# Stick-breaking heads of a hybrid block: turned weights in other PSUM banks and first in each step, two gates behind the last head, one causal select for both parts

## The chip, the cores and the metric

The kernel runs on one core of one Trainium2 chip. The metric is the device time of one execution in microseconds. Names of engines: PE multiplies matrices (PEld is its queue of weight loads, which overlaps it), DVE is the vector engine, ACT the scalar engine, POOL is GpSimd, and SP issues most DMAs. PSUM has eight banks of 128 x 512 fp32 values; matmuls write there, and ACT and DVE read it.

## What is computed

One transformer block over 512 tokens with a model width of 1024: a modulated RMS norm, then two mixers side by side (retention with 4 heads, stick-breaking attention with 16 heads of width 64), their gated sum, an output projection, a modulated feed-forward part, and a final norm. The stick-breaking mixer, retention's scores and the merge are what matters here:

```python
def stick_breaking_attention(q, k, v):
    scale = SB_HEAD_DIM ** -0.5
    for i in range(s_len // BLOCK):                  # 4 blocks of 128 queries
        end = (i + 1) * BLOCK
        z = jnp.einsum('bhtd,bhsd->bhts', qb, kb).astype(jnp.float32) * scale
        mask = s_pos[None, :] < t_pos[:, None]
        log_1m_beta = jnp.where(mask, jax.nn.log_sigmoid(-z), 0.0)
        after = lax.cumsum(log_1m_beta, axis=3, reverse=True) - log_1m_beta
        log_a = jax.nn.log_sigmoid(z) + after
        a = jnp.where(mask, jnp.exp(log_a), 0.0)
        outs.append(jnp.einsum('bhts,bhsd->bhtd', a.astype(v.dtype), vb))
...
    decay_mask = jnp.where(diff >= 0, jnp.exp(jnp.maximum(diff, 0.0) * log_gamma[:, None, None]), 0.0)
    scores = jnp.einsum('bhncd,bhnmd->bhncm', qc, kc) * decay_mask[None, :, None]
...
    g_sb, g_ret = jnp.split(jax.nn.sigmoid(br + b_branch[l]), N_BRANCH, axis=-1)
    merged = (g_sb * jnp.einsum('bse,ed->bsd', o_sb, w_proj_sb[l])
              + g_ret * jnp.einsum('bse,ed->bsd', o_ret, w_proj_ret[l]))
```

## The kernel before

Every fp32 matrix is held as two parts of a rounded type, `hi` and `lo`, and a product is three matmuls (hi hi, hi lo, lo hi). `split` (L204) makes the parts: ACT writes `hi` (L206), DVE the difference `lo` (L208, or L209 with a scale). Activations are kept with the features in the 128 partitions and the 512 tokens in the free dimension. Weights come by DMA as `raw` tiles of 128 x 1024 and are split into `whi` and `wlo`. A product of 512 x 1024 activations with 128 columns of weights (`gemm`) is 24 matmuls of 512 columns into one bank.

PSUM has three pools: `ps` with four banks, `z` with three, `av` with one. A tile of a pool can be written again once the readers of the tile that had the bank before it are done.

**Order.** The program issues instructions through a framework that orders each engine's queue by a model of when operands are there; so neighbouring pieces of code interleave in a queue. `issue_after` holds back what is in its block until the named instruction has been placed.

**Retention.** A head's scores are made by `ret_scores` (L708) into the three `z` banks, in four blocks of columns from the table `GEO`: key block j against the queries from j onward. Entry j = 3 had a block of 256 columns, of which the first 128 lie above the diagonal; both parts of every block are made by `split` (ACT, then DVE), and then `causal` (L587) sets what lies above the diagonal to zero on POOL by `affine_select` (L592): for each of three banks, hi and lo apart, 128 columns at the bank's start, and for bank 2 also 256 columns that hold j = 3's zeroed half and its diagonal block. That is eight selects a head, thirty-two in all. `ret_out` (L739) then multiplies the blocks with the values, bank by bank of the output (`z`, `z`, `z`, `av`), in matmuls that read the selected tiles. For head 0 this stands right behind the making of the sums for the later split products by `sv_acts`, a long row of DVE additions over SBUF tiles (L878, L889).

**Stick-breaking.** Sixteen heads run one behind the other in the loop over `heads(h)` (L1087); step h holds these pieces:

- `sb_front(h)`: eight matmuls of q and k into three `z` banks (two each of 512, 384, 256 and 128 columns), then eight sigmoids on ACT (L627) from these banks into SBUF: 1 - beta into `n4`, `n1`, beta into `b4`, `b1` (the tiles s and t of one of two `stick_sets`)
- `sb_turn(h - 1)`: ten PE transposes (L643) of the weights of the head before, 128 x 128 each, into three further `z` tiles, and three splits of them (ACT L206, DVE L208) into `s` tiles
- `sb_scan(h)`: DVE's products along the row, a scan of 1024 and one of 256 columns (L633) and the multiplications by beta (L634); issued behind the last split of `sb_turn`
- `sb_out(h - 1)`: eight matmuls of values and turned weights into the `av` bank, a copy out by ACT (L663), a DMA that moves 64 partitions to the other half (`t<-t`, L665), and an addition (L666) into the tile `o_sb`

Beside these, each step has work for PE that depends on no head: an odd h up to 11 has `mix(1)`, one gate of 24 matmuls (`gate`, its sigmoid `g<-ps` at L808); an even h up to 10 has `sb_qk(p)`, 48 matmuls that make q and k of two later heads; h = 12 to 15 have `mix(2)`, and h = 16, which has only the turn and the output of head 15, has none left. I call these gate steps, qk steps and two-gate steps. Behind the loop, `acts` splits the eight `o_sb` tiles, and the projection of the stick-breaking mixer multiplies all of them (`gemm(o, weight(("ps", d)), acts)`).

The order of the three pieces that use `z` banks is front, turn, next front; so three banks carry six tiles a step.

Of the kernel before, what the change touches and what calls it, by code (L numbers as in the profile page):

```python
# [15 lines left out]
ALU = mybir.AluOpType  # L16
# [3 lines left out]
P = 128  # L20
# [83 lines left out]
SM_BADA, SM_G1, SM_G2, SM_GF, SM_BB, SM_C, SM_N = 0, 48, 56, 64, 72, 88, 96  # L104


GEO = ((0, 0, 0, 512), (1, 0, 128, 384), (2, 0, 256, 256), (2, 256, 256, 256))


SEG = ((0, 1, 384, 896), (1, 2, 0, 0), (2, 1, 0, 512), (3, 0, 0, 0))  # L110
# [5 lines left out]
def kernel(  # L116
# [9 lines left out]
    nc = tc.nc  # L126
# [9 lines left out]
    def nm(s):  # L136
        uid[0] += 1
        return f"{s}_{uid[0]}"

    def ps():  # L140
        return pspool.tile([P, S], F32, tag="ps", bufs=BUFS["ps"], name=nm("ps"))

    def psa():
        return pspool.tile([P, S], F32, tag="av", bufs=BUFS["av"], name=nm("av"))

    def psz():
        return pspool.tile([P, S], F32, tag="z", bufs=BUFS["z"], name=nm("z"))

    def pair(tag):
        return apool.tile([P, 2, S], F32R, tag=tag, bufs=BUFS[tag], name=nm(tag))  # L150

    def tmp():
        return apool.tile([P, S], F32, tag="t", bufs=BUFS["t"], name=nm("t"))

    def otile():
        return apool.tile([P, S], F32, tag="o", bufs=BUFS["o"], name=nm("o"))
# [21 lines left out]
    for j in range(KT):  # L178
# [13 lines left out]
                            channel_multiplier=-1)  # L192
# [11 lines left out]
    def split(dst_hi, dst_lo, src, scale=1.0, eng=None):  # L204

        nc.scalar.activation(dst_hi, src, AF.Copy, scale=scale)  # L206
        if isinstance(scale, float) and scale == 1.0:
            return (eng or nc.vector).tensor_sub(dst_lo, src, f(dst_hi))  # L208
        return nc.vector.scalar_tensor_tensor(  # L209
            dst_lo, src, scale, f(dst_hi), op0=ALU.mult, op1=ALU.subtract  # L210
        )
# [15 lines left out]
    def mm(o, lhs, rhs, start, stop):  # L227
        return nc.tensor.matmul(o, lhs, rhs, start=start, stop=stop, skip_group_check=True).ins  # L228

    def mm3(o, lh, ll, rh, rl, start, stop):  # L230
        mm(o, lh, rh, start, False)
        mm(o, lh, rl, False, False)
        mm(o, ll, rh, False, stop)
# [206 lines left out]
    with tc.manual_schedule(engines={nc.vector.engine, nc.scalar.engine, nc.tensor.engine}):  # L440

        nc.scalar.preload_act_table_set("natural_log_exp_and_others")
        c = sm[:, SM_C : SM_C + KT]
# [137 lines left out]
    def sb_qk(p):  # L581
        qp, kp = ps(), ps()
        gemm(qp, weight(("sq", p)), hs)
        gemm(kp, weight(("sk", p)), hs)
        sb_qk_store(p, qp, kp)

    def causal(t, bank):  # L587

        op = ALU.is_ge

        def sel(ap, n, base):
            nc.gpsimd.affine_select(  # L592
                ap, ap, pattern=[[1, n]], compare_op=op, fill=0.0, base=base,
                channel_multiplier=-1,
            )

        sel(t[:, 0:P], P, 0)
        if bank == 2:
            sel(t[:, 256:512], 256, -P)

    def sticks():

# [10 lines left out]
    def sb_front(h):  # L613
        q, k = sbq[h], sbk[h]
        z = [psz(), psz(), psz()]
        for i, bank, c, _ in reversed(SEG):
            w = (i + 1) * P
            for n in range(2):
                head_pe[h] = mm(z[bank][:, c : c + w], q[:, n, i * P : (i + 1) * P], k[:, 0:w],
                                n == 0 and c == 0, n == 1)  # L620
        n4, n1, b4, b1 = stick_sets[h % 2]
        for segs in ((3,), (2, 0), (1,)):
            for (t4, t1), scale in (((n4, n1), -1.0), ((b4, b1), 1.0)):
                for i, bank, c, at in (SEG[i] for i in segs):
                    w = (i + 1) * P - 1
                    t = t1 if i == 1 else t4
                    nc.scalar.activation(t[:, at : at + w], z[bank][:, c : c + w], AF.Sigmoid, scale=scale)  # L627
        return n4, n1, b4, b1

    def sb_scan(n4, n1, b4, b1):  # L630
        for n, b, d in ((n4, b4, diag), (n1, b1, diag[:, 640:896])):
            w = n.shape[-1]
            nc.vector.tensor_tensor_scan(n[:, ::-1], n[:, ::-1], d[:, ::-1], 0.0, op0=ALU.mult, op1=ALU.max)  # L633
            nc.vector.tensor_mul(b[:, 0 : w - 1], b[:, 0 : w - 1], n[:, 1:w])  # L634

    def sb_turn(n4, n1, b4, b1):
        at = [psz(), psz(), psz()]
        for i, _, _, a in reversed(SEG):
            t = b1 if i == 1 else b4
            for j in range(i + 1):  # L640
                bank, c = TGEO[j]
                c += (i - j) * P
                nc.tensor.transpose(at[bank][:, c : c + P], t[:, a + j * P : a + (j + 1) * P], ident)  # L643
        avs = []
        for bank in range(3):
            w = TBANKW[bank]
            hl = pair("s")
            ins = split(hl[:, 0, :w], hl[:, 1, :w], at[bank][:, :w])
            avs.append(hl)
        return avs, ins  # L650

    def sb_out(h, avs):
        vt = sbv[h // 4]
        o = psa()
        r, hf = (h % 4) // 2, h % 2
        for j in (3, 2, 1, 0):
            bank, c = TGEO[j]
            w = S - j * P
            v = vt[j // 2][:, j % 2, r * 256 + hf * P : r * 256 + hf * P + P]
            for i in range(2):  # L660
                mm(o[:, j * P : S], v, avs[bank][:, i, c : c + w], j == 3 and i == 0, j == 0 and i == 1)
        u, u2 = tmp(), tmp()
        nc.scalar.activation(u, o, AF.Copy)  # L663
        own, oth = (slice(0, HD), slice(HD, P)) if hf == 0 else (slice(HD, P), slice(0, HD))
        nc.sync.dma_start(u2[own], u[oth])  # L665
        nc.vector.tensor_add(o_sb[h // 2][own], u[own], u2[own])  # L666
# [41 lines left out]
    def ret_scores(h, qk):  # L708
        q1, q2, k1, k2 = qk
        z = [psz(), psz(), psz()]  # L710
        st = {}
        for j in (3, 2, 1, 0):
            bank, c, t0, w = GEO[j]
            js = slice(j * P, (j + 1) * P)
            for n, (q, k) in enumerate(((q1, k1), (q2, k2))):
                mm3(z[bank][:, c : c + w], k[:, 0, js], k[:, 1, js], q[:, 0, t0:S], q[:, 1, t0:S],
                    n == 0 and j != 2, n == 1)
        for j in (3, 2, 1, 0):
            bank, c, t0, w = GEO[j]
            if bank not in st:  # L720
                st[bank] = pair("s")
            hl = st[bank]
            split(hl[:, 0, c : c + w], hl[:, 1, c : c + w], z[bank][:, c : c + w],
                  gk[:, h * 4 + j : h * 4 + j + 1])
        for bank in (2, 1, 0):
            for i in range(2):
                causal(st[bank][:, i, :], bank)
        return st

    def ret_scale(h, ssq):  # L730
# [8 lines left out]
    def ret_out(h, st, vt):  # L739
# [3 lines left out]
        for b, o in enumerate(banks):  # L743
            for j in range(b + 1):
                bank, c, t0, _ = GEO[j]
                at = c + b * P - t0
# [297 lines left out]
    qk = ret_qk(0, qk_ps)  # L1044
    vt = ret_v(v_ps)
    st = ret_scores(0, qk)
    sgs = ret_silu(0)
    steps = sv_acts()
# [4 lines left out]
    for h in range(3):  # L1053
        ys = ret_gate(h, *outs, sgs)
        qk = ret_qk(h + 1)
        st, outs = {}, []
        vt = lambda: [rvts[b] for b in range(4)]
        seven(("vg", h + 1), h, lambda: ys, rv_store, lambda: st.update(ret_scores(h + 1, qk)),
              lambda: outs.extend(ret_out(h + 1, st, vt())))
        sgs = [rsgs[b] for b in range(4)]  # L1060
# [6 lines left out]
    def sb_v(g):  # L1067

        sbv[g] = [pair("v") for _ in PI]
        for n, vt in enumerate(sbv[g]):  # L1070
            nc.sync.dma_start(f(vt), vspill[2 * (g - 2) + n])

    sbv.update({g: [vts[g, n] for n in PI] for g in PI})
    mixes = [(ret_mix, d) for d in range(8)] + [(sb_mix, d) for d in range(8)]

    def mix(n):
        for _ in range(n):
            fn, d = mixes.pop(0)
            fn(d)
# [5 lines left out]
    fronts = {}  # L1085

    def heads(h):  # L1087
        with tc.issue_after(act_table.ins):
            ins = act_table
            if h < 16:  # L1090
                fronts[h] = sb_front(h)
            if h:
                if h % 8 == 1 and h > 8:
                    sb_v(2)
                    sb_v(3)
                avs, ins = sb_turn(*fronts.pop(h - 1))
            if h < 16:
                with tc.issue_after(ins.ins):
                    sb_scan(*fronts[h])
            if h:  # L1100
                if h % 2:
                    o_sb[h // 2] = otile()
                sb_out(h - 1, avs)

    for h in range(17):
        heads(h)
        p = h // 2 + 2
        if p > 7:
            mix(min(2, len(mixes)))
        elif h % 2:  # L1110
            mix(1)
        else:
            sb_qk(p)
# [7 lines left out]
    for d in range(8):  # L1121
        o = ps()
        gemm(o, weight(("ps", d)), acts)
        r, t = tmp(), tmp()
# [5 lines left out]
        ins = split(hl[:, 0, :], hl[:, 1, :], t)  # L1130
# [596 lines left out]
```

## Time and profile before

| | us |
|---|---|
| median of 3 runs | 1130.73 (1130.22 to 1131.09) |
| the profiled execution's own time | 1131.71 |
| its span, first to last instruction | 1129.8 |
| heads, first front to the last output | about 474 to 687 in the span |

The profile's mean granted PE clock is 0.997 of full speed. One row of the instruction timeline is: start in us, duration in us, engine, line, operation, output and inputs by the program's names, partitions x elements, count; in brackets the engine's idle time before it and what ended it. A row that stands for several instructions of one kind has their common duration. PE's durations overlap (a matmul's end is modelled and includes its way through the array), so what a matmul costs is read from start to start.

### The profile page before, as it was taken

To read this page: it belongs to the slowest core of one execution; us is meant where nothing else is said; L and a number is where in the kernel's file an instruction comes from. 1 tells how busy PE (TensorE), PEld (TensorE's weight loads), DVE (VectorE), ACT (ScalarE), POOL (GpSimd) and SP (SyncE) were. 2 spreads that over 40 slices of the span, in tenths; PEclk is the share of its full clock that TensorE was granted. 3 is DMA by queue.
4 is the path that set the end of the run, shared out by engine and by line. 5 is a ranking of instruction groups with operands and counts; after the bars stand their busy time and mean duration, and the time that the engine had idled before them with its cause. 6 is when DMAs were issued, how large, how long until landed. Compare 5 with 4: busy or idle time off the path is not lost.

```text
span 1129.8 us, 15925 instructions
## 1 busy us (share of the span) xinstructions
PE 1112.0 (98%) x6096; PEld 958.7 (85%) x6096; DVE 837.8 (74%) x1174; ACT 554.1 (49%) x863; POOL 65.9 (6%) x94
## 2 busy tenths in 40 slices
PE   8999999999999999999999999999999999999996
PEld 6887888888888888877777777889999999999986
DVE  7898856959968958476777765767996777667656
ACT  5445445435434644355555553357655444444333
POOL 0031000011021010000000000000000000000000
PEclk9999999999999999999999999999999999999998
DMA  9714432766776476867675448762556564564322
GB/s 357 297 56 150 146 115 87 224 133 209 233 159 224 141 162 237 219 172 203 163 203 164 124 129 297 249 185 57 151 186 165 171 169 112 149 186 132 92 77 75
DMA packets 63147, 190.90 MB, mean 169 GB/s; under 512 B 7776, under 2 KB 9824, under 8 KB 63072
## 3 DMA queue, kind: packets, MB, share of 16 engines
q1 hardware_dynamic: 55760, 171.02, 47.1%
q0 software_dynamic: 6768, 18.35, 9.5%
q8 instruction: 48, 0.79, 0.3%
q10 hardware_dynamic: 544, 0.52, 0.1%
q14 instruction: 27, 0.22, 0.1%
HBM read 146.35 MB, written 16.78 MB: 144 GB/s over the span
## 4 chain that ended last, share of the span: by engine, by line
PE 86%; DVE 5%; ACT 3%; DMA 3%; issue 2%; POOL 1%; SPq 0%; DVEq 0%; ACTq 0%
PE ps L228 65%; PE z L228 15%; PE av L228 3%; PE z L643 2%; ACT s L627 1%; POOL s L592 1%; DMA araw<-wada 1%; DVE araw L256 1%; DMA sraw<-wada 1%; ACT g L808 1%; DVE wlo L859 1%; DVE wlo L208 0%; DMA q<-qp 0%; DVE t L766 0%; DMA t<-t 0%
## 5 line engine op out<-in xcount | busy, mean ns | idle before, releaser
L228 PE MATMUL ps<-h,whi 128*128 128x512 f32 (+1 forms) x1154 | 339.9, 376 | 0.0
L228 PEld LDWEIGHTS ps<-h,whi 128*128 128x128 f32 x1154 | 209.1, 189 | 34.7 <-issue 0.5
L228 PE MATMUL ps<-h,wlo 128*128 128x512 f32 (+1 forms) x577 | 215.3, 377 | 0.0
L206 ACT ACTIVATE whi<-raw 128x1024 fp32r<-128x1024 f32 (+1 forms) x104 | 108.5, 1044 | 183.2 <-PE ps L228 137.4
L208 DVE TENSOR_TENSOR wlo<-raw,whi 128x1024 fp32r<-128x1024 f32 (+1 forms) x104 | 125.0, 1203 | 72.8 <-ACT whi L206 72.0
L228 PE MATMUL ps<-s,whi 128*128 128x512 f32 x480 | 148.8, 391 | 1.4 <-ACT s L206 1.0
L228 PEld LDWEIGHTS ps<-h,wlo 128*128 128x128 f32 x577 | 108.9, 189 | 17.1
L228 PE MATMUL z<-q,whi 128*128 128x256 f32 x504 | 106.8, 283 | 0.0
L228 PEld LDWEIGHTS ps<-s,whi 128*128 128x128 f32 x480 | 89.3, 188 | 20.1 <-ACT s L206 1.5
L859 DVE TENSOR_TENSOR wlo<-s,whi 128x1024 fp32r<-128x1024 f32 x46 | 56.1, 1223 | 53.2 <-ACT whi L855 53.1
L228 PE MATMUL ps<-s,wlo 128*128 128x512 f32 x240 | 93.5, 389 | 0.0
L228 PEld LDWEIGHTS z<-q,whi 128*128 128x128 f32 x504 | 84.9, 192 | 1.5
L855 ACT ACTIVATE whi<-s 128x1024 fp32r<-128x1024 f32 x47 | 49.7, 1057 | 59.0 <-PE ps L228 48.5
L228 PE MATMUL ps<-whi,h 128*128 128x512 f32 x222 | 71.4, 391 | 0.0
L1168 DVE SCALAR_TENSOR_TENSOR o<-ps,mod,o 128x512 f32<-128x512 f32 (+1 forms) x63 | 42.5, 681 | 33.7 <-PE ps L228 33.6
L208 DVE TENSOR_TENSOR s<-z,s 128x512 fp32r<-128x512 f32 (+1 forms) x60 | 33.6, 614 | 27.6 <-ACT s L206 27.6
L228 PEld LDWEIGHTS ps<-s,wlo 128*128 128x128 f32 x240 | 45.1, 188 | 9.4
L855 ACT ACTIVATE whi<-raw 128x1024 fp32r<-128x1024 f32 x28 | 29.6, 1058 | 47.0 <-PE ps L228 45.2
L228 PEld LDWEIGHTS ps<-whi,h 128*128 128x128 f32 x222 | 41.6, 188 | 9.5 <-ACT t L999 0.6
L228 PE MATMUL ps<-q,whi 128*128 128x256 f32 (+1 forms) x224 | 49.3, 314 | 0.0
L228 PE MATMUL z<-qp,whi 128*128 128x256 f32 x168 | 47.3, 283 | 0.0
L228 PE MATMUL z<-q,wlo 128*128 128x256 f32 x168 | 46.4, 283 | 0.0
(320 smaller groups left out, 2127.2 us busy)
## 6 DMA issues: line engine op xcount, KB each, us to landing
raw<-wp SPq DMA_DIRECT2D x145, 512.0 KB, 4.0
araw<-wada SPq DMA_DIRECT2D x32, 512.0 KB, 4.0
araw<-wp SPq DMA_DIRECT2D x30, 512.0 KB, 4.3
s<-wp SPq DMA_DIRECT2D x24, 512.0 KB, 6.1
sraw<-wada SPq DMA_DIRECT2D x16, 512.0 KB, 8.6
q<-qp SPq DMA_DIRECT2D x32, 256.0 KB, 3.7
spill<-o POOLq DMA_DIRECT2D x24, 256.0 KB, 5.0
o<-xT SPq DMA_DIRECT2D x16, 256.0 KB, 4.1
```

The lines of the kernel that those rows point to most:

```text
L206: nc.scalar.activation(dst_hi, src, AF.Copy, scale=scale)
L208: return (eng or nc.vector).tensor_sub(dst_lo, src, f(dst_hi))
L228: return nc.tensor.matmul(o, lhs, rhs, start=start, stop=stop, skip_group_check=True).ins
L256: nc.vector.scalar_tensor_tensor(raw, raw, 1.0, cact, op0=ALU.mult, op1=ALU.mult, accum_out=col)
L592: nc.gpsimd.affine_select(ap, ap, pattern=[[1, n]], compare_op=op, fill=0.0, base=base, channel_multiplier=-1,)
L627: nc.scalar.activation(t[:, at : at + w], z[bank][:, c : c + w], AF.Sigmoid, scale=scale)
L643: nc.tensor.transpose(at[bank][:, c : c + P], t[:, a + j * P : a + (j + 1) * P], ident)
L808: nc.scalar.activation(g, o, AF.Sigmoid, bias=sm[:, SM_BB + i : SM_BB + i + 1])
L855: nc.scalar.activation(hi, t, AF.Copy)
L859: nc.vector.tensor_sub(lo, t, f(hi))
L1168: return nc.vector.scalar_tensor_tensor(x1[d][:, hv], o[:, hv], mod[:, gcol + d : gcol + d + 1], x1[d][:, hv], op0=ALU.mult, op1=ALU.add,)
```

## The change

It has four parts. `causal` is now one select for each key block j, over 128 columns of hi and lo together (a 128 x 2 x 128 view), called for j = 3, 2, 1, 0 in the reverse order of `GEO`; and j = 3's block holds 128 columns in place of 256, so the zeroed half is neither made nor selected. `sb_turn` takes two banks of the `ps` pool and the `av` bank in place of three `z` banks. In `heads`, the turn comes first, then front and scan of the head, no longer held behind the turn's split. And the last eight gates, which `mix` takes from its list, are dealt 1, 2, 2, 1, 2 to h = 12 to 16 in place of 2, 2, 2, 2, 0, so that two gates stand behind the last head's turn.

```diff
-GEO = ((0, 0, 0, 512), (1, 0, 128, 384), (2, 0, 256, 256), (2, 256, 256, 256))
+GEO = ((0, 0, 0, 512), (1, 0, 128, 384), (2, 0, 256, 256), (2, 256, 384, 128))
...
-    def causal(t, bank):
-
-        op = ALU.is_ge
-
-        def sel(ap, n, base):
-            nc.gpsimd.affine_select(
-                ap, ap, pattern=[[1, n]], compare_op=op, fill=0.0, base=base,
-                channel_multiplier=-1,
-            )
-
-        sel(t[:, 0:P], P, 0)
-        if bank == 2:
-            sel(t[:, 256:512], 256, -P)
+    def causal(t, c):
+
+        ap = t[:, :, c : c + P]
+        nc.gpsimd.affine_select(
+            ap, ap, pattern=[[0, 2], [1, P]], compare_op=ALU.is_ge, fill=0.0, base=0, channel_multiplier=-1
+        )
...
     def sb_turn(n4, n1, b4, b1):
-        at = [psz(), psz(), psz()]
+        at = [ps(), ps(), psa()]
...
-        for bank in (2, 1, 0):
-            for i in range(2):
-                causal(st[bank][:, i, :], bank)
+        for bank, c, _, _ in reversed(GEO):
+            causal(st[bank], c)
...
     def heads(h):
         with tc.issue_after(act_table.ins):
             ins = act_table
-            if h < 16:
-                fronts[h] = sb_front(h)
             if h:
...
                 avs, ins = sb_turn(*fronts.pop(h - 1))
             if h < 16:
-                with tc.issue_after(ins.ins):
-                    sb_scan(*fronts[h])
+                fronts[h] = sb_front(h)
+                sb_scan(*fronts[h])
...
         if p > 7:
-            mix(min(2, len(mixes)))
+            mix((1, 2, 2, 1, 2)[h - 12])
```

What the change moves in the queues is shown at three places. Numbers behind a name tell tiles of one name apart; a row with a count at its end stands for instructions in a row.

PE, in a step with a gate or qk product (`h` and `whi`, `wlo` are that product's operands, `con,s` and `con,t` the transposes, `q` the front, `av` the output), before:

```order
L228 MATMUL z_4270<-q_4023,q_4024 128x256 x2
L228 MATMUL z_4269<-q_4023,q_4024 128x128 x2
L228 MATMUL ps_4327<-h_209,whi_4331 128x512 x2
L228 MATMUL ps_4327<-h_209,wlo_4332 128x512
L228 MATMUL ps_4327<-h_250,whi_4331 128x512 x2
L643 MATMUL z_4287<-con,s_3833 128x128 x2
L643 MATMUL z_4287<-con,t_3834 128x128
L643 MATMUL z_4287<-con,s_3833 128x128
L228 MATMUL ps_4327<-h_250,wlo_4332 128x512
L228 MATMUL ps_4327<-h_297,whi_4331 128x512
L643 MATMUL z_4288<-con,s_3833 128x128 x3
L643 MATMUL z_4288<-con,t_3834 128x128
```

The same place of the changed kernel, from the last transposes of the step on:

```order
L636 MATMUL ps_4390<-con,t_3810 128x128
L636 MATMUL ps_4391<-con,t_3810 128x128
L636 MATMUL ps_4390<-con,s_3809 128x128
L228 MATMUL z_4412<-q_4007,q_4013 128x512 x2
L228 MATMUL z_4413<-q_4007,q_4013 128x384 x2
L228 MATMUL z_4414<-q_4007,q_4013 128x256 x2
L228 MATMUL z_4413<-q_4007,q_4013 128x128 x2
L228 MATMUL ps_4450<-h_209,whi_4453 128x512 x2
L228 MATMUL ps_4450<-h_209,wlo_4454 128x512
```

The transposes stood behind the front in three groups between matmuls of the product, bank by bank; now all ten stand together ahead of the front.

POOL, retention's head 0, before (s_638 is block j = 0, s_635 j = 1, s_630 holds j = 2 and 3):

```order
L592 AFFINE_SELECT s_630<-s_630 128x256 x2
L592 AFFINE_SELECT s_635<-s_635 128x128 x2
L592 AFFINE_SELECT s_638<-s_638 128x128 x2
L592 AFFINE_SELECT s_630<-s_630 128x128 x2
```

And of the changed kernel:

```order
L590 AFFINE_SELECT s_630<-s_630 128x2x128
L590 AFFINE_SELECT s_635<-s_635 128x2x128
L590 AFFINE_SELECT s_638<-s_638 128x2x128
L590 AFFINE_SELECT s_630<-s_630 128x2x128
```

Eight instructions became four, in the same order of blocks (3, 1, 0, 2).

DVE, in `sv_acts` beside these selects (`h` and `s` are tiles in SBUF; `wlo` a weight's low part), before:

```order
L208 TENSOR_TENSOR wlo_940<-raw_937,whi_939 128x1024
L208 TENSOR_TENSOR wlo_970<-raw_967,whi_969 128x1024
L889 TENSOR_TENSOR q_808<-s_782,q_807 128x1024
L889 TENSOR_TENSOR qp_820<-s_781,qp_819 128x1024
L878 TENSOR_TENSOR s_782<-h_391,s_782 128x256
```

And of the changed kernel:

```order
L208 TENSOR_TENSOR wlo_936<-raw_933,whi_935 128x1024
L881 TENSOR_TENSOR q_804<-s_778,q_803 128x1024
L208 TENSOR_TENSOR wlo_966<-raw_963,whi_965 128x1024
L870 TENSOR_TENSOR s_778<-h_391,s_778 128x256
L870 TENSOR_TENSOR s_778<-h_438,s_778 128x256
L870 TENSOR_TENSOR s_778<-h_486,s_778 128x256
L870 TENSOR_TENSOR s_778<-h_525,s_778 128x256
L881 TENSOR_TENSOR qp_816<-s_777,qp_815 128x1024
```

The subtraction into `q`, which stood behind both weights' low parts, now stands between them, and four additions moved ahead of the one into `qp`. ACT's copy that the subtraction into `q` waits for moved as well: it stood behind the load of the silu table and four silus, and stands ahead of that load now.

## The prediction

> **What bounds the kernel now.** First the profile page's engine totals and its chain of work that ended last, to learn which engine to follow:
>
> ```profile
> span 1129.8 us, 15925 instructions
> PE 1112.0 (98%) x6096; PEld 958.7 (85%) x6096; DVE 837.8 (74%) x1174; ACT 554.1 (49%) x863; POOL 65.9 (6%) x94
> PE 86%; DVE 5%; ACT 3%; DMA 3%; issue 2%; POOL 1%; SPq 0%; DVEq 0%; ACTq 0%
> ```
>
> PE is busy for 98% of the span and carries 86% of the chain. An edit off PE is worth something only where PE stands still for it, or is slowed. What a matmul costs I take from the chain's long stretches, start to start:
>
> ```profile
> 104.27 58.37 PE ps L228 x257
> 162.64 3.87 PE z L228 x24
> 815.95 2.87 PE z L228 x24
> 681.52 1.09 PE z L643 x10
> ```
>
> The first gives 58.37 / 257 = 0.227 us for 512 columns, the third 2.87 / 24 = 0.120 for 256, the last 0.109 for a transpose. Now the heads, in PE's timeline; two steps with a boundary at each front (`z<-q,q`):
>
> ```profile
> 510.95 1.37 PE L228 MATMUL z<-q,q 128*128 128x512 f32 x8
> 512.16 0.67 PE L228 MATMUL ps<-h,whi 128*128 128x512 f32 x2
> ...
> 512.90 0.40 PE L228 MATMUL ps<-h,whi 128*128 128x512 f32 x1
> 513.49 0.44 PE L643 MATMUL z<-con,s 128*128 128x128 f32 x2 [0.19 <-ACT s L627]
> ...
> 516.12 0.33 PE L228 MATMUL av<-s,v 128*128 128x128 f32 x1
> 516.29 0.44 PE L228 MATMUL ps<-h,whi 128*128 128x512 f32 x1
> ...
> 517.26 1.32 PE L228 MATMUL av<-s,v 128*128 128x128 f32 x7
> 518.42 0.40 PE L228 MATMUL ps<-h,wlo 128*128 128x512 f32 x1
> ...
> 520.72 1.37 PE L228 MATMUL z<-q,q 128*128 128x512 f32 x8
> ...
> 535.91 1.37 PE L228 MATMUL z<-q,q 128*128 128x512 f32 x8
> ```
>
> The gate step takes 520.72 - 510.95 = 9.77 us. Its matmuls need 24 x 0.227 = 5.45 for the gate, 1.09 for ten transposes, 512.16 - 510.95 = 1.21 for the front, and about 1.22 for the eight output matmuls (two each of 128 to 512 columns: 2 x (0.062 + 0.120 + 0.174 + 0.227) = 1.17 by column count, plus 0.05 for changing over): 8.97. So 0.80 is lost. The qk step takes 535.91 - 520.72 = 15.19 and needs 48 x 0.227 + 3.52 = 14.42: 0.77 lost. Where it goes is in the rows. The transposes write the banks that the front has just filled, so they must wait until the sigmoids have read them: at 512.90 a gate matmul of 0.23 starts, and PE next starts at 513.49, 0.36 late, released by ACT's sigmoid. The two further groups wait in the same way for less, and three groups and a split output (one matmul, then seven) mean more changes of operand. In the stage's rows grouped by line the weight loads of these transposes carry the sum of the wait:
>
> ```profile
> L643 PEld LDWEIGHTS z<-con,s 128*128 128x128 f32 x120 | 13.7, 140 | 13.8 <-ACT s L627 12.8
> ```
>
> That is 12.8 us over the 15 steps that have both a front and a turn, 0.85 each, somewhat more than PE loses, since a waiting load is partly hidden behind a matmul.
>
> **The change: heads.** With the turn in `ps` and `av` banks and first, the transposes need no sigmoid of their own step. What is late next? I put the changed order on a clock that starts with the first transpose, with durations from these rows of ACT and DVE:
>
> ```profile
> 521.66 0.67 ACT L808 ACTIVATE g<-ps,sm 128x512 f32<-128x512 f32 x1
> 522.23 2.16 ACT L627 ACTIVATE s<-z 128x511 f32<-128x511 f32 x6
> 524.23 0.71 ACT L627 ACTIVATE t<-z 128x255 f32<-128x255 f32 x2
> 524.75 1.44 ACT L206 ACTIVATE s<-z 128x512 fp32r<-128x512 f32 x3
> ...
> 515.61 1.62 DVE L208 TENSOR_TENSOR s<-z,s 128x512 fp32r<-128x512 f32 x3 [1.77 <-ACT s L206]
> 517.15 2.28 DVE L633 TENSOR_TENSOR_SCAN s<-s,table 128x1024 f32<-128x1024 f32 x1
> 519.35 0.67 DVE L633 TENSOR_TENSOR_SCAN t<-t,table 128x256 f32<-128x256 f32 x1
> 519.93 1.20 DVE L634 TENSOR_TENSOR s<-s,s 128x1023 f32<-128x1023 f32 x1
> 521.05 0.42 DVE L634 TENSOR_TENSOR t<-t 128x255 f32<-128x255 f32 x1
> ```
>
> PE: transposes until 1.09, front until 2.30, then six to ten product matmuls, so the output would start at 3.7 to 4.6. ACT now makes the three splits first: from about 1.3 to 2.75, then the sigmoids to 5.6. DVE's three differences run behind ACT's, to 3.6 to 3.9. The output writes the one `av` bank, which the turn's third tile holds until DVE's third difference: it comes just in time with nine or ten product matmuls ahead of it, and up to 0.3 late with six. The scan of 1024 needs four sigmoids (about 4.3), runs to 6.7, the short one to 7.3, and the weights `b4` are ready at 8.4 and `b1` at 8.8. The next transposes come at 9.1 at the earliest; seven of ten need only `b4`. So no wait remains in the sum, with 0.7 us to spare in a gate step. I leave 0.18 a step for the change-overs and the short waits for `av`: 0.80 - 0.18 = 0.62, times 15 steps = **-9.3 us**. Bounds: -5 (half of each step's loss stays) and -10.5 (0.70 a step).
>
> **The last head.** Before, its output DMA has only the projection's start as cover:
>
> ```profile
> 692.21 0.39 PE L228 MATMUL ps<-s,whi 128*128 128x512 f32 x1
> 693.64 0.74 PE L228 MATMUL ps<-s,whi 128*128 128x512 f32 x2 [1.04 <-ACT s L206]
> ...
> 687.10 4.98 DMA t<-t
> ```
>
> PE stands still for 693.64 - 692.21 - 0.227 = 1.20 us. Now 48 gate matmuls, 10.9 us, stand beside the output, and the projection's 21 matmuls of the first seven tiles (4.8 us) still stand ahead of the first that needs the last tile. The DMA's 4.98 us and about 1.5 for addition and split end within them: **-1.2**. The gates moved here leave h = 12 and 15 as steps with one gate; their cover is the 9.1 us above. If the cover failed, 1.2 us would come back.
>
> **The narrower block.** Four heads times six matmuls of 256 columns become 128. A front's own 128-column pair shows what those cost: 1.21 - 2 x (0.227 + 0.174 + 0.120) = 0.17 for two, with a late start of the next, so about 0.11 each against 0.120. That is 24 x 0.01 = **-0.2 us**. By column count (0.062) it would be -1.4. I take the row's. The Trainium skill ("TensorE: Matmul & The Clock Gate", LDWEIGHTS) says that loading a 128-column stationary operand takes columns / 1.2, 107 ns, whatever the moving operand; its rule and the 0.11 agree.
>
> **Causal selects.** Here one select is on the chain. The row of the selects by form, then POOL and PE, and DVE's row of work beside them:
>
> ```profile
> L592 POOL TENSOR_SCALAR_AFFINE_SELECT s<-s x32: 282/298/12691, 74.3 to 364.0; 128x128 fp32r<-128x128 f32 x24, 128x256 fp32r<-128x256 f32 x8
> ...
> 76.08 12.69 POOL L592 TENSOR_SCALAR_AFFINE_SELECT s<-s 128x128 fp32r<-128x128 f32 x1
> ...
> 86.84 0.61 PE L228 MATMUL z<-v,s 128*128 128x512 f32 x2
> 88.82 3.92 PE L228 MATMUL z<-v,s 128*128 128x512 f32 x16 [1.37 <-POOL s L592]
> ...
> 76.08 1.08 DVE L878 TENSOR_TENSOR s<-h 128x256 f32<-128x256 f32 x3
> ...
> 86.26 2.36 DVE L208 TENSOR_TENSOR wlo<-raw,whi 128x1024 fp32r<-128x1024 f32 x2
> 89.38 1.23 DVE L889 TENSOR_TENSOR q<-s,q 128x1024 fp32r<-128x1024 f32 x1 [0.76 <-ACT q L888]
> ```
>
> A select that normally takes 0.29 us began at 76.08, when DVE began a row of instructions with two SBUF inputs without a gap. DVE's first gap is at 86.26 + 2.36 = 88.62; the select ended at 76.08 + 12.69 = 88.77, 0.15 later. PE lost 88.82 - 86.84 - 2 x 0.227 = 1.5 us. So the select got nothing until DVE paused. In the changed order this costs more. Three of the four selects fit ahead of the row (I put the third's start 0.25 us before it), the fourth (j = 2) does not; and the gap at 88.62 goes, since ACT's copy `q` is made early. DVE's row goes on through `q` (1.23), four additions, `qp`, four more and a low part: about 6.1 us more by these rows, less some 1.0 because the row starts earlier (j = 3 is shorter), so it pauses at 88.62 + 6.1 - 1.0 = 93.7. There DVE needs ACT behind an output bank that PE cannot finish without the select. PE has 15 matmuls of the output free of it: from 86.84 to 90.25. It then waits to about 93.9 (the pause, the 0.15, and 0.05 to start), 3.6 us, where it lost 1.5 before: **+2.1 us**. Bounds: -1.5 (the select gets in early, stall gone) and +4.3 (the third select is caught too: PE waits from 86.84 until DVE first needs an ACT result behind this output, the last low part at 93.7 - 1.1 = 92.6, so 5.8 - 1.5). I take the middle case, as the row shows a select held through some 36 instructions.
>
> A rule of the Trainium skill speaks of this place: by "SBUF — State Buffer" (Who interferes with whom), a two-input DVE instruction and a GpSimd instruction that reads SBUF exclude each other, and the one that comes second is blocked until the first has finished. The exclusion agrees with the 12.69 us; that it ends with one DVE instruction does not agree with this row.
>
> **The sum.** 1131.7 (the profiled execution) - 9.3 - 1.2 - 0.2 + 2.1 = 1123.1. The shown median lies 1.0 below that execution, so I forecast **1122.1 us**.
>
> **Rivals.**
> (a) The fourth select gets in early, because DVE's row has a gap or frees it between two instructions. For it: ACT's copy into `qp` may come a few tenths too late for DVE, which opens a gap. Against it: the 12.69. Then the term is -1.5: 1122.1 - 3.6 = 1118.5.
> (b) Two selects are caught: +4.3 instead of +2.1, 1124.3. For it: only 0.25 us separates the third from the row.
> (c) The heads keep most of their loss, because the wait only moves: the output to the third difference (one `av` bank) and the sigmoids behind the splits. With 0.15 of 0.62 gained, -2.3 in place of -9.3: 1129.1. For it: the third difference comes within 0.3 of the output. Against it: ACT has 9 us a step for about 6 of work.
> (d) Slower: the transposes, now first, wait for `b4`. The scan chain starts later than before, behind the turn's splits on ACT and differences on DVE, and nothing of its step is left ahead of the next transposes to hide a delay. The spare time is 0.7 us; beyond it each tenth costs every gate step a tenth. Only the eight steps with one gate are short enough to bite, the others have more to spare. Without the heads' gain the forecast is 1131.4; to come to 1133.5 these eight must lose 9.3 + 2.1 = 11.4, 1.4 each, so the chain must be 0.7 + 1.4 = 2.1 us later than I laid it out. Nothing in the rows is that late, as DVE is 74% busy.
> (e) That it does not do what it says: the queue order shows the ten transposes together and first, so only that the waits are not where I put them, which is (c).
>
> **How the numbers follow.** A difference under 0.2% (2.3 us) can hardly be told from no change, so faster means below 1128.5 and slower above 1133.0. Chances: forecast 0.50, (a) 0.22, (b) 0.11, (c) 0.12 (a third of it faster), (d) 0.05. Faster 0.50 + 0.22 + 0.11 + 0.04 = 0.87; same 0.08; slower 0.05. The range reaches from (a) with the heads' -10.5, 1118.5 - 1.2 = 1117.3, to (b) with -5, 1124.3 + 4.3 = 1128.6; I give 1117.3 to 1128.5. It leaves out (d) and most of (c).
>
> **What would show it.** In the changed trace: gate steps of about 9.15 us and qk steps of about 14.6 from the first transpose to the next, with no wait for ACT's sigmoids in front of a transpose; no wait of PE for the last tile's split behind the heads; at retention's head 0 a select of j = 2 of some 18 us, and PE waiting about 3.6 us for POOL near 90 to 94. The prediction is wrong if transposes wait for DVE's L634 row (b4, b1), if the output waits for a difference by more than 0.3 us a step, or if the selects all take 0.3 to 0.5.

## The result, and the profile after

| | before | after |
|---|---|---|
| median, us | 1130.91 (4 runs, 1130.22 to 1131.85) | 1121.76 (4 runs, 1121.00 to 1123.74) |
| ratio, 95% interval | | 0.9921 (0.9904 to 0.9938) |
| span of the profiled execution | 1129.8 | 1119.3 |

The changed kernel is faster by 0.8%, 9 us, and the forecast of 1122.1 us hit the time. Two of its terms did not hold: they were wrong in opposite directions, so that the sum came this close is in part luck. The page's first rows, and the chain by engine:

```profile
span 1119.3 us, 15918 instructions
PE 1105.4 (99%) x6096; PEld 961.4 (86%) x6096; DVE 836.9 (75%) x1174; ACT 553.7 (49%) x863; POOL 50.8 (5%) x78
PE 93%; DVE 4%; issue 1%; DMA 1%; SPq 0%; ACT 0%; DVEq 0%; ACTq 0%
```

PE's share of the chain rose from 86 to 93%; ACT and POOL, which had 3 and 1%, are gone from it. To see where the time went, the kernel is cut at two points of PE's timeline that both kernels have: the first front (`z<-q,q`), and a row of 84 matmuls behind the merge, from which on both take the same time. First before, then after; each time PE's timeline at the first front and the chain at the later point:

```profile
473.79 0.96 PE L228 MATMUL z<-q,q 128*128 128x512 f32 x4
...
767.26 10.07 PE ps L228 x84
```

```profile
472.29 0.96 PE L228 MATMUL z<-q,q 128*128 128x512 f32 x4
...
756.77 10.07 PE ps L228 x84
```

The heads, the gates behind them and the start of the projection take 284.5 us in place of 293.5: **-9.0**. Ahead of the first front **-1.5** is gained in these two profiles; that point lies between 472.3 and 475.4 in the six profiles that keep the old selects, so the difference by itself shows nothing of the selects, and their own place is shown further down. The forecast had -10.5 (-9.3 and -1.2) for the first and +1.9 (+2.1 and -0.2) for the second.

**The heads after.** PE's timeline from one turn to the next but one:

```profile
508.34 0.38 PE L636 MATMUL ps<-con,s 128*128 128x128 f32 x2
...
509.35 1.47 PE L228 MATMUL z<-q,q 128*128 128x512 f32 x8
510.66 0.67 PE L228 MATMUL ps<-h,whi 128*128 128x512 f32 x2
...
512.55 0.39 PE L228 MATMUL ps<-h,wlo 128*128 128x512 f32 x1
512.89 1.51 PE L228 MATMUL av<-s,v 128*128 128x128 f32 x8
514.24 0.62 PE L228 MATMUL ps<-h,whi 128*128 128x512 f32 x2
...
517.68 0.38 PE L636 MATMUL ps<-con,s 128*128 128x128 f32 x2
...
522.35 1.43 PE L228 MATMUL av<-s,v 128*128 128x128 f32 x8
...
532.24 0.38 PE L636 MATMUL ps<-con,s 128*128 128x128 f32 x2
```

No transpose waits for ACT any more: in the whole stage PE has no idle time ahead of one that the profile shows. The gate step takes 517.68 - 508.34 = 9.34 us (9.77 before, 9.15 forecast), the qk step 14.56 (15.19 before, 14.6 forecast). What is left of the gate step's loss is in three places: the front behind the transposes takes 510.66 - 509.35 = 1.31 where it took 1.21, the output begins 512.89 - 512.55 - 0.227 = 0.11 late, and its eight matmuls take 514.24 - 512.89 = 1.35 where the sum had 1.22. DVE's multiplication by beta in that step:

```profile
515.45 1.20 DVE L627 TENSOR_TENSOR s<-s,s 128x1023 f32<-128x1023 f32 x1
```

`b4` is ready at 515.45 + 1.20 = 516.65, 8.3 us into the step (8.4 forecast) and 1.0 ahead of the next transposes.

**Head 0 of retention after.** PE, POOL and DVE beside the selects, then PE at the next transposes:

```profile
86.95 4.24 PE L228 MATMUL z<-v,s 128*128 128x512 f32 x18
...
93.75 0.62 PE L228 MATMUL ps<-h,whi 128*128 128x512 f32 x2
...
75.02 0.95 POOL L590 TENSOR_SCALAR_AFFINE_SELECT s<-s 128x256 fp32r<-128x256 f32 x2 [0.25 <-DVE s L209]
...
75.26 1.32 DVE L870 TENSOR_TENSOR s<-h 128x256 f32<-128x256 f32 x3
...
98.64 0.33 PE L762 MATMUL z<-con,t 128*128 128x128 f32 x1 [0.42 <-DVE t L758]
```

The third select began 0.24 us ahead of DVE's row, as laid out (75.02 and 75.26). The fourth did not wait for the row: both were done at 75.97, and three DVE additions took 1.32 us in place of 1.08, so DVE waited for POOL. PE's 18 output matmuls run without a stop. Of the 1.5 us, 0.58 comes back at once: PE reaches the next transposes before DVE's scaled product (start 98.64, where 98.06 was possible).

### The profile page after: what moved, and what is told of

Read it like the earlier page. It is cut to its first block, busy times and chain, and to the rows that moved or that the text cites. A ratio compares the mean times of both kernels' runs of the same rounds, so it can differ in the third digit from the quotient of the medians.

```text
span 1119.3 us, 15918 instructions
## 1 busy us (share of the span) xinstructions
PE 1105.4 (99%) x6096; PEld 961.4 (86%) x6096; DVE 836.9 (75%) x1174; ACT 553.7 (49%) x863; POOL 50.8 (5%) x78
## 4 chain that ended last, share of the span: by engine, by line
PE 93%; DVE 4%; issue 1%; DMA 1%; SPq 0%; ACT 0%; DVEq 0%; ACTq 0%
PE ps L228 70%; PE z L228 17%; PE av L228 3%; PE ps L636 1%; DVE s L870 1%; DVE wlo L208 1%; DMA sraw<-wada 1%; PE z L762 1%; DVE t L758 0%; PE av L636 0%; SPq L180 0%; DVE t L1033 0%; DVE q L881 0%; DVE s L209 0%; DVE fin L1603 0%
## 5 line engine op out<-in xcount | busy, mean ns | idle before, releaser
L228 PE MATMUL ps<-h,whi 128*128 128x512 f32 (+1 forms) x1154 | 334.3, 374 | 0.0
L228 PE MATMUL ps<-h,wlo 128*128 128x512 f32 (+1 forms) x577 | 212.9, 372 | 0.0
L228 PE MATMUL z<-qp,wlo 128*128 128x256 f32 x160 | 45.3, 283 | 0.0
```

## The experiments

Single profiles of this program differ by a microsecond or two ahead of the heads, whatever the kernel: PE's wait for DVE near 287 us was 0.25 us in seven of thirteen profiles and up to 1.7 in the others. So stages are compared, and times only where several runs were made. "Stage" is the stretch between the two points above (before 293.5, after 284.5).

### Both halves of the change apart

`heads_only` is the changed kernel with the old `GEO`, `causal` and its eight calls; `causal_only` is the kernel before with the new ones:

```diff
+GEO = ((0, 0, 0, 512), (1, 0, 128, 384), (2, 0, 256, 256), (2, 256, 384, 128))
...
+        for bank, c, _, _ in reversed(GEO):
+            causal(st[bank], c)
```

> The changed kernel with the causal selects and GEO of before: heads and last gates alone. Theory A (the parts add up, as the two traces have it: heads about -7.8 us, last head -1.4): about 1130.9 - 9.2 = 1121.7, and retention's head 0 keeps its select of about 12.7 us and PE's wait of 1.5 us. Rival B (the heads gain 0.62 in each of 15 steps as forecast, and the select part is worth nothing): about 1120.4.

> The kernel before with the new causal selects and GEO alone. Theory A: the 1.5 us wait at retention's head 0 goes, 0.6 of it comes back as a wait of the next transposes for DVE, the narrower blocks give 0.15, the wait near 386 loses up to 0.36: -1.1 to -1.5, so 1129.4 to 1129.8. Rival B (the new selects cost as I forecast, +2.1): 1132.8. Heads as before, about 0.8 us lost in each of 15 steps.

Measured: heads alone 1123.40, ratio 0.9923 (0.9906 to 0.9939), stage 285.0; its selects, eight in each of four heads, had the long one again:

```profile
L592 POOL TENSOR_SCALAR_AFFINE_SELECT s<-s x32: 284/298/12689, 76.3 to 365.2; 128x128 fp32r<-128x128 f32 x24, 128x256 fp32r<-128x256 f32 x8
```

The selects alone: 1132.38, ratio 1.0000 (0.9988 to 1.0012), stage 292.9. The longest of sixteen selects took 1.34 us:

```profile
L590 POOL TENSOR_SCALAR_AFFINE_SELECT s<-s x16: 402/407/1337, 75.0 to 362.2; 128x256 fp32r<-128x256 f32 x16
```

So the whole measurable gain is that of the heads and the moved gates. The selects take away the 1.5 us stall, and 0.58 comes back; about a microsecond is left in that stage, which the total time doesn't show. My +2.1 for them is refuted; the -1.1 to -1.5 expected of this run lies at the edge of what the interval allows (0.9988 is -1.4 us).

### Which part of the heads

`banks_only` and `order_only` are each one part put into the kernel before:

```diff
-        at = [psz(), psz(), psz()]
+        at = [ps(), ps(), psa()]
```

```diff
-            if h < 16:
-                fronts[h] = sb_front(h)
...
             if h < 16:
-                with tc.issue_after(ins.ins):
-                    sb_scan(*fronts[h])
+                fronts[h] = sb_front(h)
+                sb_scan(*fronts[h])
```

> The kernel before with the turn in two ps banks and the av bank, nothing else: front still first, scan still behind the turn's split. Theory A (the loss came from banks alone: transposes waiting for the sigmoids of the banks that the front had just filled): no transpose waits for ACT, ten in one group, 0.5 to 0.55 us less a step, so -7.5 to -8.3 in all, last head as before. Rival (the order matters, the transposes must stand ahead of the front): a wait moves to the front or the output, and under half of it, less than 4 us, is gained.

> The kernel before with the turn first in each step and the scan no longer held, but still in z banks. Now the front writes banks that the turn's splits must have read, and stands behind some eight product matmuls. Theory A: the wait of transposes for sigmoids goes, and the front in the middle of the product brings two more change-overs and a wait for DVE's differences of 0.1 to 0.3: a gain of 0.2 to 0.4 a step, -3 to -6 us in all. Rival (banks are what matters, so the wait only moves from the transposes to the front): within 1.5 us of before.

> The changed kernel once more, as the measure for the others of this chip: 0.992 of the kernel before, about 9 us.

Measured on one chip, with the ratio to the kernel before:

```
             median    ratio (95%)               stage
after_again  1122.81   0.9910 (0.9893 - 0.9926)  284.7
banks_only   1128.98   0.9968 (0.9953 - 0.9982)  290.6
order_only   1132.97   1.0009 (0.9996 - 1.0022)  295.7
```

Neither part does it alone: -2.9 and +2.2 in the stage, where both (with the moved gates) make -8.8. With the new banks alone, PE's timeline and then ACT's and DVE's show the wait in another place:

```profile
516.11 0.39 PE L228 MATMUL ps<-h,whi 128*128 128x512 f32 x1
516.78 0.41 PE L228 MATMUL av<-s,v 128*128 128x128 f32 x2 [0.28 <-DVE s L208]
...
511.77 2.17 ACT L627 ACTIVATE s<-z 128x511 f32<-128x511 f32 x6
513.77 0.71 ACT L627 ACTIVATE t<-z 128x255 f32<-128x255 f32 x2
514.30 1.17 ACT L206 ACTIVATE s<-ps 128x512 fp32r<-128x512 f32 x2
...
516.22 0.41 DVE L208 TENSOR_TENSOR s<-av,s 128x256 fp32r<-128x256 f32 x1
```

The transposes run through, but ACT has the front's sigmoids ahead of the turn's splits, so DVE's last difference ends at 516.63, and the output waits 516.78 - 516.11 - 0.227 = 0.44 us for it in this gate step (0.29 in the qk step). With the new order alone, at the end of a gate step, PE's timeline and DVE's:

```profile
519.32 0.39 PE L228 MATMUL ps<-h,wlo 128*128 128x512 f32 x1
520.86 0.42 PE L643 MATMUL z<-con,s 128*128 128x128 f32 x2 [1.15 <-DVE s L634]
...
519.49 1.23 DVE L634 TENSOR_TENSOR s<-s,s 128x1023 f32<-128x1023 f32 x1
```

Here the front writes the `z` banks that the turn has just used. The queue has it behind ten product matmuls in a gate step and twelve in a qk step, and the scan ends too late: the transposes behind each of the six gate steps start 1.3 us late. From turn to turn a gate step takes 10.6 us (the first 11.0; 9.77 before) and a qk step 14.7 (15.19 before). That is the mechanism of the prediction's rival (d), in gate steps as it said, but in this kernel and not in the changed one. Theory A fell in both runs. The rivals' numbers came true (under 4 us gained; within 1.5 us of before), for the order by another way than expected: the wait is not at the front, it is at the next transposes. As far as these two runs show, the transposes have to stand ahead of the front so that their splits come ahead of the sigmoids, and they need other banks so that the front can follow them at once. `order_only` also lets the scan go, as the change does; no run has that alone. In both runs retention's long select went through (see below), which is in their totals and not in the stage.

### The gates behind the last head

`mix_old` deals the last gates as before:

```diff
-            mix((1, 2, 2, 1, 2)[h - 12])
+            mix(min(2, len(mixes)))
```

> The changed kernel with the last gates dealt as before (two each at h = 12 to 15, none behind the last head). If the gates behind the last head are what took its wait away, PE waits again 0.5 to 1.2 us for the last tile's split, and for the output bank 0.1 to 0.2: +0.7 to +1.4 against the changed kernel. If the changed order had already ended it: no wait and no difference.

```profile
685.26 0.72 PE L228 MATMUL ps<-s,whi 128*128 128x512 f32 x2 [0.76 <-ACT s L206]
```

The wait for the last tile's split is back (0.92 us from start to start), and the stage takes 286.2, 1.5 more than the changed kernel on that chip; 1123.78, ratio 0.9922 (0.9902 to 0.9943). So the trace bears out the forecast's 1.2; the totals of this run and of the changed kernel overlap in their intervals.

### What held the select

The forecast put the fourth select behind DVE's whole row. In the changed kernel it went through. Two kernels start it later still, further inside the row: `dup_select` does block j = 0 twice, `gap_select` puts two memsets ahead of it.

```diff
             causal(st[bank], c)
+            if h == 0 and bank == 0:
+                causal(st[bank], c)
```

```diff
+            with tc.issue_after(sel.ins):
+                sel = nc.gpsimd.memset(gap, 0.0)
+                sel = nc.gpsimd.memset(gap, 0.0)
+            with tc.issue_after(sel.ins):
+                causal(st[2], 0)
```

> The changed kernel with the select of block j = 0 of retention's head 0 done twice (the second changes nothing), so that the select of j = 2 starts about 0.55 us later, inside DVE's row of two-input additions and right behind a running select. Theory T1 (a select waits for the DVE instruction that runs, not for the row, as long as POOL has one queued behind the other): last select about 0.6 us, time within 0.5 us of the changed kernel's 1121.8. Theory T2 (a select that starts inside the row waits for DVE's next pause): last select about 18 us, PE waits about 4 us near 90, time about 1126.

> The changed kernel with two POOL memsets of a spare tile between the third and the fourth select of retention's head 0, so that the fourth starts inside DVE's row with no select ahead of it that reads SBUF. T1: the fourth select about 0.4 to 0.9 us, time within 0.5 us of 1121.8. T2: about 18 us, PE waits about 4 us near 90 for POOL, time about 1126.

Measured: 1124.56 and 1122.27 in one run each. At head 0 the longest selects inside the row took 0.59 and 0.64 us; nothing waited for POOL there. T1's select times hold, for these; its time holds for `gap_select` and is missed by 2.8 us in `dup_select`. (What `dup_select` loses lies elsewhere: against the changed kernel's profile, 3.6 us shorter, 1.7 stand ahead of the first selects and 1.4 in the heads.) That leaves the 12.7 us before. `eight_shift` is the kernel before with one memset ahead of the two selects of j = 0; `tie_probe` adds a row of DVE additions with 87 selects beside it behind the end of the kernel before.

```diff
+            with tc.issue_after(ins.ins):
+                ins = nc.gpsimd.memset(gap, 0.0)
+            with tc.issue_after(ins.ins):
+                for i in range(2):
+                    ins = causal(st[0][:, i, :], 0)
```

```diff
+        for n in range(220):
+            nc.vector.tensor_add(o[:, 0:256], x[:, 0:256], y[:, 0:256])
...
+        for n in range(48, 392, 8):
+            pick()
+            nc.gpsimd.memset(gap[:, 0:n], 0.0)
```

> The kernel before, its eight selects, with one POOL memset of a spare tile ahead of the two selects of block j = 0 of retention's head 0, so that the select that was held starts some 0.15 us later against DVE's row (which it met within 4 ns of the start of a DVE instruction in both profiles that show it). T3 (a select is held for the whole row only if it starts within a few ns of a DVE instruction; else it waits for one instruction): no select over 1.4 us at head 0, no wait of PE for POOL there. T4 (the form matters: 128 x 128 of one part is held in a row of two-input instructions, 128 x 2 x 128 is not): again a select of about 12.5 us and PE's 1.5 us wait.

> The kernel before with a measurement put behind its end: a row of 220 two-input DVE additions of 128 x 256 without a gap, beside it on POOL 43 selects of 128 x 128, each followed by a memset that is 8 columns longer each time, then 22 pairs of selects. The starts of the selects so move through the period of 0.335 us in steps of about 8 ns. T3: most selects take 0.3 to 0.75 us, as they wait for one addition, and one that meets a start within a few ns is held to the end of the row, tens of us. T4: the first select inside the row is held to its end. Neither (all take under 0.8 us): what held the select before needs something else than the row and the start. The time is that of before plus about 75 us of the row.

With the shift, POOL's timeline:

```profile
76.69 0.32 POOL L732 MEMSET gap<- 128x256 f32 x1
76.95 1.58 POOL L592 TENSOR_SCALAR_AFFINE_SELECT s<-s 128x128 fp32r<-128x128 f32 x4
```

Four selects of the same form, the last three begun inside the same DVE row, take 1.58 us together, and PE's wait for POOL is gone. The select that had been held now starts 0.08 us later against DVE (85 ns behind an addition in place of 3). So the form is not it (T4 falls), and neither is the row. In the probe (1233.82 us with its row), the selects by form, and ten of DVE's additions without a select beside them:

```profile
L1674 POOL TENSOR_SCALAR_AFFINE_SELECT q<-q x87: 286/331/625, 1124.6 to 1166.9; 128x128 fp32r<-128x128 f32 x87
...
1199.80 4.57 DVE L1672 TENSOR_TENSOR t<-t,t 128x256 f32<-128x256 f32 x10
```

None of 87 took more than 0.34 us over the shortest. But the probe does not make the row that it was meant to make. Its additions start 0.46 us apart and are 0.43 long, so DVE pauses for 0.03 us behind each, and the row lasts 106 us in place of 75; in the row that held the select they start 0.335 apart and are 0.42 long, without a pause. One select began 4 ns behind the start of an addition: it took 0.29 us, and the addition 0.57. So T3 fails here, but in a row with pauses, and for a row without them the probe decides nothing.

The other runs tell more. Five kernels have the eight old selects and the same order of instructions on POOL and DVE at this place: the kernel before, `heads_only`, `tie_probe` (which has the kernel before ahead of its row), `banks_only` and `order_only`. POOL in the last three, in this order (the first row is the select ahead of it and the held one):

```profile
75.63 12.93 POOL L592 TENSOR_SCALAR_AFFINE_SELECT s<-s 128x128 fp32r<-128x128 f32 x2
...
75.74 1.66 POOL L592 TENSOR_SCALAR_AFFINE_SELECT s<-s 128x128 fp32r<-128x128 f32 x4
...
75.30 1.66 POOL L592 TENSOR_SCALAR_AFFINE_SELECT s<-s 128x128 fp32r<-128x128 f32 x4
```

In three the same select took 12.69 us, and in two 0.56, beside the same row. So neither the order nor the row makes it by itself. What differs in the records is a few nanoseconds: the select starts 3, 4 and 2 ns behind the row's first addition where it was held, 7 and 6 ns where it was not, and 85 ns, as said, in `eight_shift`. That is in keeping with T3, but five kernels with one profile each do not show it, and no run moved that start alone. What holds a select through a row stays open.

### Two attempts at the rest

What is left in a gate step stands around the output. `splits_back` makes the turn's splits in the order in which their banks are done, `ps3` takes a third `ps` bank for the turn and leaves `av` to the output:

```diff
-        for bank in range(3):
+        for bank in (2, 1, 0):
...
-            avs.append(hl)
+            avs.insert(0, hl)
```

```diff
-        at = [ps(), ps(), psa()]
+        at = [ps(), ps(), ps()]
```

> The changed kernel with the turn's three splits in the order av bank, second, first (the order in which the transposes finish the banks), so that the output can start one difference of 0.69 us earlier. If the output's start behind the last difference is what is left of the loss in gate steps (0.1 to 0.3), 0.1 less in each of 15 steps, about 1121.0 where the changed kernel has 1122.3. If the change-overs are what is left, or the output now waits for the last bank's split: the same or up to 2 us slower.

> The changed kernel with the turn's third bank in ps too, so that the output's bank is free and its first matmul needs only the second split, not the third. The output is put three or four product matmuls earlier, in one matmul and seven. If the single av bank holds up the output in the changed kernel (0.1 to 0.2 in steps behind a gate and in two-gate steps), 1 to 1.5 us less than it. If the output now waits for the difference that it needs, as with the splits turned round, 2 to 4 us more.

Measured: 1126.23, ratio 0.9935 (0.9921 to 0.9949), stage 287.2; and 1128.64, ratio 0.9963 (0.9951 to 0.9976), stage 290.5. Both are slower than the changed kernel in the stage, by 2.6 and 5.8 us, against 284.5 to 284.7. In both the order that comes out puts the output some matmuls earlier, in one and seven, and it waits there: in the gate steps of `splits_back` for DVE's difference, 0.3 us,

```profile
630.38 0.30 PE L228 MATMUL av<-s,v 128*128 128x128 f32 x1 [0.28 <-DVE s L208]
```

and in `ps3` for ACT's, about 0.3 us a step from start to start, and once a gate step a product matmul waits for a `ps` bank that DVE has not read yet (0.34). Both edits also moved the output in the queue, so neither shows what the `av` bank by itself costs. No run was clearly faster than the changed kernel.

## Why the prediction was right

Point by point, by the prediction's own steps:

- **What bounds the kernel**: right that PE's stalls are what can be won; the rows of ACT and POOL left the chain. Their share of it was not the gain: 3 and 1% of 1129.8 are some 45 us, and the time fell by 9, of the some 15 us that PE had lost at the places of the forecast (15 steps of 0.8, 1.2 and 1.5).
- **Heads, -9.3**: the mechanism was right, a size was off. Of -9.0 in the stage, 1.5 belong to the moved gates (`mix_old`), so the heads brought about -7.5. The step that was mis-sized is "I leave 0.18 a step for the change-overs and the short waits for `av`": the gate step kept 9.34 - 8.97 = 0.37 and the qk step 14.56 - 14.42 = 0.14. The two-gate steps kept more than half of their 0.77: they went from 15.19 (fronts at 635.79 and 650.98, before) to 14.84 (transposes at 637.26 and 652.10, after), -0.35 in place of -0.62. Of the gate step's 0.37, the front's 0.10 and the output's 0.11 and 0.13 make 0.34. In a two-gate step the output stands behind six product matmuls and begins 641.22 - 640.78 - 0.227 = 0.21 late; the prediction's own clock had "up to 0.3 late with six", which its 0.18 a step has no room for beside the change-overs. The value lies inside the bounds of -5 and -10.5.
- **What is late next**: the clock of the changed step was right to a tenth where it was checked (`b4` at 8.3 for 8.4). `order_only` shows what that margin was worth: with `b4` late, PE waits 1.3 us behind each of six gate steps and the gain is gone.
- **The last head, -1.2**: right (1.5 with the output's wait).
- **The narrower block, -0.2**: in keeping with the trace. The 24 matmuls of retention's scores take 3.81 us in place of 3.87, in a head:

```profile
161.74 3.81 PE z L228 x24
```

  0.06 for six narrower matmuls, 0.01 each, as the front's pair had said, and not the 0.058 each of the column count. The prediction's 0.11 is the spacing of the matmuls, and only that agrees with the load time that it set beside it; the weight loads' own records are 140 ns long in its row of L643.
- **Causal selects, +2.1**: wrong; rival (a) took place, -1.5, with 0.58 handed back. The step that failed is "Three of the four selects fit ahead of the row (I put the third's start 0.25 us before it), the fourth (j = 2) does not", together with "I take the middle case, as the row shows a select held through some 36 instructions". The first half was exact: the third began 0.24 before the row, the fourth inside it. That a select inside the row is held until the row pauses was read from one case, and it is not what a row does: in five profiles (`after`, `causal_only`, `dup_select`, `gap_select`, `eight_shift`) selects inside such a row took 0.47 to 0.64 us, and in `banks_only` and `order_only` so did the very select that the prediction had seen held. The prediction set the rule of the Trainium skill ("SBUF — State Buffer", Who interferes with whom: the second is blocked until the first instruction has finished) aside for that one row; these profiles agree with the rule, and only the held select (in three kernels) does not.
- **The sum** came out within 0.4 us, and that is in good part luck. The heads brought 1.8 us less and the selects cost 3 us less than forecast, the last head brought 0.3 more; 0.36 of retention's last wait came on top (at 386.47 before; it varies from profile to profile), and the four runs of the changed kernel are themselves 2.7 us apart. The time alone would have hidden both errors.

## What to carry to other kernels

Giving a stage other banks and moving it to the front of its step are one edit: either alone moved the wait to the next place (the output's bank, the scan) and won a third or nothing. After such an edit, follow each engine's queue for a whole step, also what stands behind what on ACT and DVE, and check the margin of the value that the next step needs first. Where a stall in the trace is one case, look whether a small shift of its start ends it before a price is built on it, and whether other kernels with the same order have it.

## What the hardware showed besides

A select that met a running row of two-input DVE instructions also held DVE up: in the probe, additions of 0.43 us became up to 0.57 us long, and beside the changed kernel's fourth select one took 0.62 in place of 0.41. One select of the old form was held for 12.69 us through a row without pauses, in three kernels (the kernel before, `heads_only`, `tie_probe`), and was not in two others with the same order (`banks_only`, `order_only`), where it started 2 to 5 ns later against DVE; its cause is not known. A 128 x 2 x 128 select takes 0.41 us, two of 128 x 128 take 0.58 to 0.60.
